# A decoder block with two-level expert routing: 160 tokens' experts gathered by row, sums over eight expert tiles, and the second norm moved into the operands

## The chip, the cores and the metric

The kernel runs on one core of a Trainium2 chip. The metric is the device time of one execution in microseconds (us); the median of the runs counts. TensorE (PE in the profile) multiplies matrices, VectorE (DVE), ScalarE (ACT) and GpSimd (POOL) work element by element, SyncE (SP) and POOL issue the transfers.

## The reference

There are 520 tokens (512 of a prompt and 8 samples) of width 2048, in fp32. A normalized input is projected, two kinds of windowed attention with gates follow, and the branches are joined and projected by `w_out`. The last part, which the change is about, is a layer of 16384 small experts, each one row of `u` and one row of `v`:

```
h = x + (sigmoid(ga) * ya + sigmoid(gb) * yb) @ w_out
hn = rmsnorm(h, norm2_w)
q = (hn @ wq).reshape(t, 8, 2, 64)            # 8 heads, two halves
s = einsum('thcd,cnd->thcn', q, subkeys)      # 128 scores for each half
half_s, half_i = top_k(s, 16)
best_s, best_c = top_k(all 256 sums of two halves, 16)
experts = i1 * 128 + i2;  gates = softmax(best_s)
act = gelu(einsum('cd,ced->ce', hn, u[experts]))
y = h + einsum('ce,ced->cd', gates * act, v[experts])
```

Each token thus uses 8 x 16 = 128 of the 16384 experts.

## The kernel before, in words

**Number format.** A weight tile of 128 x 2048 fp32 (1 MB) is fetched by SP into one of two raw buffers. In two halves of 1024 columns ACT rounds it to fp32r (`wh`, L297) and DVE subtracts to get the rest (`wl`, L299). Each product is three matmuls: wh with the rounded operand, wh with its rest, wl with the rounded operand. All matmuls of this kind have line L336. `plan` lists the weights in order, and `stream` starts the next tile's transfer and splitting one tile ahead.

**Stages.** By the trace's time: projections and attention until about 975 us; the branches until 1143; `wout` until 1389; the query products `wq` with the routing until 1826; the gates until 2179; the rest of the dense `u` tiles that are stored until 2286; then the experts until 3890. The last four hold the two ways in which expert products are made:

- *Dense*, for the first ND = 392 tokens. PE multiplies all 16384 rows: `u_tile` makes 128 experts x 392 tokens from 16 x 3 matmuls of 392 columns, a norm factor is multiplied in by DVE (L930), and ACT takes the gelu. The first 70 of the 128 tiles are computed while routing and gates run, and stored to DRAM (`act_d`); the rest are computed among the `v` products. The gates are spread out to a dense matrix by `build_g`: for every four tokens DVE compares indices with an iota (`eA`, `Bt`, L1097 and L1099), POOL and ACT multiply in the gate (`AA`), and PE makes the outer products (`gq`, L1080); it is stored as `g_d`. In the experts `c_tile` multiplies a tile by its gates (L1218) and splits it (`cb`, L1221). `v_group` sums GRP = 4 tiles in PSUM, for two chunks of 128 of the output's width at a time, and DVE adds the sum to `acc` (L1263).
- *Gathered*, for the last NS = 128 tokens. With one token on each partition, an indirect DMA of POOL fetches a row of `u` for each (128 x 2048, 1 MB, L1155); DVE multiplies it with the token and sums (`dot`, L1185). After 128 of these come 128 rows of `v`, which DVE adds with a weight (`add`, L1197). Three buffers take turns. At the end PE transposes the sums.

**Norm.** Before, HH and HL hold h times the norm's weight without the factor 1/rms. The factor `rstd` is made after the first query product and multiplied in where a product leaves PSUM.

**What sets the order.** Everything else is hung on PE's work: each matmul counts its columns, and each 16 x 260 columns is a *tick*. A tick advances one of up to three generators (top-16 searches, `build_g`, `gathered`); PACE = 3.1 is the ticks between two gathered rows. PE and SP run in the order of the code, in the experts POOL too; a scheduler places the instructions of the other engines. top-16 (`best_all`) runs token tile by token tile: the gathered tile of 128 first, then four of 98.

Of the kernel before, what the change touches and what calls it, by code (L numbers as in the profile page):

```python
# [49 lines left out]
KA = 12  # L50
NEXP = 128
NSPILL = 70
GRP = 4
TICK = 16
NACT = 3
COPY_EVERY = 9
# [3 lines left out]
NCB = 6  # L60
NGB = 3
PACE = 3.1
PRE = 2
LEAD = 3
# [27 lines left out]
def _layout(a):  # L92
# [12 lines left out]
    o["v"] = f["peer_v"][0].reshape(NEXP // GRP, GRP, P, 4, 2, 256).transpose(0, 3, 2, 4, 1, 5)  # L105
# [46 lines left out]
def _plan():  # L152
    p = [("win", 8 + i) for i in range(4)] + [("win", i) for i in range(8)]
    for j in range(NJ):
        for g in range(NG):
            p += [("win", b + g * 4 + j) for b in (12, 24, 36)]
    p += [("win", 48 + i) for i in range(32)]
    for c in range(0, KC, 2):
        p.append(("wba", c // 2))
        if c % 4 == 0:  # L160
            p.append(("wbb", c // 4))
    p += [("wout", i) for i in range(KC)] + [("wq", i) for i in range(PH)]
    p += [("uT", i) for i in range(NSPILL)]
    for g in range(NEXP // GRP):
        p += [("uT", i) for i in range(g * GRP + (g > 0), min(NEXP, g * GRP + GRP + 1)) if i >= NSPILL]
        p += [("v", (g, q)) for q in range(4)]
    return p


def _program(tc, I, O):  # L170
# [16 lines left out]
    onesR = cp.tile([P, P], F32R, name="onesR")  # L187
    V.tensor_copy(onesR, ones)
# [5 lines left out]
    eg = cp.tile([P, 2, P], F32, name="eg")  # L194
# [31 lines left out]
    act_d = dp.tile([NSPILL, P, ND], F32, name="act_d")  # L226
    g_d = dp.tile([NGC, P, NK, GC], F32, name="g_d")


    clock = {"n": 0}  # L230
    first, active, queue = deque(), deque(), deque()

    def soon(f, lag=1):
        first.append((clock["n"] + lag, f))

# [20 lines left out]
    def drain(all_=True):  # L256
        while first:
            first.popleft()[1]()
        while all_ and (active or queue):
            step()  # L260
# [161 lines left out]
    qk = sp = tab = sbias = qs = kn = vn = None  # L422
# [3 lines left out]
    def start_attention():  # L426
        nonlocal qk, sp, tab, sbias, qs, kn, vn
# [3 lines left out]
        sp = at.enter_context(tc.tile_pool(name="sp", bufs=1))  # L431
        tab = sp.tile([P, 512], F32, name="tab")
# [382 lines left out]
    oa = (lambda k: sl["OA"][:, k], lambda k: sl["OA"][:, 8 + k])  # L815
# [21 lines left out]
    for n in range(2):  # L837
        for c in range(KC):
# [35 lines left out]
    acc = slp.tile([P, KC, T], F32, name="acc", tag="S2")  # L874
    HHt = slp.tile([P, KC, ND], F32R, name="HH", tag="S3")
    HGt = slp.tile([P, KC, NS], F32R, name="HG", tag="S3g")
    ssq = bt.tile([P, T], F32, name="ssq")
    for c in range(KC):
        w = stream(("wout", c))
        if c < 4:  # L880
            S_.dma_start(acc[:, c * 4:c * 4 + 4, :], I["xT"][:, c * 4:c * 4 + 4, :])
        ps = psum_mm()
        dot3(ps, w, (mH, mL))
        V.tensor_tensor(v2(acc[:, c]), v2(acc[:, c]), ps[:, :, :TH], op=OP.add)
        w2 = cst[:, C_N2 + c:C_N2 + c + 1]
        A.activation(HHt[:, c], acc[:, c, :ND], AF.Copy, scale=w2)
        A.activation(HGt[:, c], acc[:, c, ND:], AF.Copy, scale=w2)
        if c == 0:
            A.activation(ssq, acc[:, c], AF.Square)
        else:  # L890
            s = tmp0()
            A.activation(s, acc[:, c], AF.Square)
# [4 lines left out]
    hg = (whole(HGt), whole(HLGt))  # L897
    for c in range(KC):
        w2 = cst[:, C_N2 + c:C_N2 + c + 1]
        V.scalar_tensor_tensor(HLt[:, c], acc[:, c, :ND], w2, HHt[:, c], op0=OP.mult, op1=OP.subtract)  # L900
        V.scalar_tensor_tensor(HLGt[:, c], acc[:, c, ND:], w2, HGt[:, c], op0=OP.mult, op1=OP.subtract)


    def q_product(h):
        w = stream(("wq", h))
        ps = psum_mm()
        terms([(ps[:, 0, :ND], 0, ND), (ps[:, 1, :NS], ND, T)],
              [pick(w, k * P) + tuple((d(k), g(k)) for d, g in zip(hw, hg)) for k in range(KC)])
# [29 lines left out]
    def spill_u():  # L938
        nonlocal nu
        act = u_tile(nu)  # L940
        G_.dma_start(act_d[nu], act)
# [7 lines left out]
    s1b = cp.tile([TT, 4096], F32, name="s1b", tag="S1b")  # L949
    hs = s1b[:, :HN].rearrange("p (t h c k) -> p t h c k", t=NTT, h=PH, c=2)  # L950
    hi = s1b[:, HN:2 * HN].bitcast(U32).rearrange("p (t h c k) -> p t h c k", t=NTT, h=PH, c=2)
    s1b0 = 2 * HN
    hf = s1b[:, s1b0:s1b0 + 256].rearrange("p (h c k) -> p h c k", h=PH, c=2)
    ab = s1b[:, s1b0 + 256:s1b0 + 512].bitcast(U32).rearrange("p (c x) -> p c x", c=2)
    abf = s1b[:, s1b0 + 768:s1b0 + 1024].rearrange("p (c x) -> p c x", c=2)
    pos_ = s1b[:, s1b0 + 512:s1b0 + 640]
    res = s1b[:, s1b0 + 1024:s1b0 + 1408].rearrange("p (c h k) -> p c h k", c=3, h=PH)
    qT = cp.tile([P, PH, T], F32, name="qT", tag="S1a")
# [11 lines left out]
    def halves_top(h):  # L970
        yield

        def score(t):
            t0, m = TILES[t]
            ps = sc_p.tile([P, 512], F32, name="sc")
            PE.matmul(ps[:m, :256], qT[:, h, t0:t0 + m], sk, start=True, stop=True)  # L976
# [16 lines left out]
    def best_all():  # L993
        s1a = cp.tile([TT, 4096], F32, name="s1a", tag="S1a")
# [16 lines left out]

        nxt = cand(0)
        yield
        yield
        for t in range(NTT):
            cur = nxt
            t0, m = TILES[t]
            for h in range(PH):
                top16(bs[:m, h], bc[:m, h * TOPK:(h + 1) * TOPK], cur[:, h], NC_)
                yield  # L1020
            if t + 1 < NTT:
# [34 lines left out]
            ps = sc_p.tile([P, 512], F32, name="sc")  # L1056
            for x in range(3):
                PE.transpose(ps[:, x * P:x * P + m], rows[:, x], ident[:m, :m])
            ts = slice(t0, t0 + m)
            V.tensor_copy(i1T[:, ts], ps[:, 0:m])  # L1060
            V.tensor_copy(i2T[:, ts], ps[:, P:P + m])
            A.activation(gH[:, ts], ps[:, 2 * P:2 * P + m], AF.Copy)
            V.tensor_tensor(gL[:, ts], ps[:, 2 * P:2 * P + m], gH[:, ts], op=OP.subtract)
            yield
        queue.append(build_g())


    def build_g():
# [257 lines left out]
```

## Time and profile before

| | |
|---|---|
| median of 3 runs | 3904.21 us (3903.19 to 3906.29) |
| profiled execution | 3891.22 us, its span 3889.5 us |
| PE busy | 3812.2 us (98%), 25080 matmuls |
| DVE, ACT, POOL busy | 2753.0 us (71%), 1436.4 us (37%), 930.5 us (24%) |
| TensorE's granted clock, mean | 0.993 of full speed |
| moved by DMA | 901.37 MB, mean 232 GB/s |

The profiled execution is 13.0 us below the median. The shares of busy time are means over stages that differ, so a stage's own window is to be read beside them. A busy PE is an engine with a matmul in flight. Durations of one instruction on DVE and POOL include the time in which it was held after its start.

### The profile page before, as it was taken

The numbers are of one execution on the slowest core, as the hardware profiler recorded it, in microseconds if no ns is written. First come the engines' busy times: TensorE is split into PE (matmuls) and PEld (weight loads), VectorE is DVE, ScalarE is ACT, GpSimd is POOL, SyncE is SP. The second block draws the span as 40 slices with busy tenths as digits, with TensorE's granted clock in tenths as the row PEclk, the third lists the DMA queues.
The fourth block names the chain that finished last, engine by engine and source line by source line (L and its number), as shares of the span: only waits on it lengthen the run. The fifth ranks groups of instructions, "written<-read, shape, count | busy, mean of one in ns | idle before, by whom it ended". The sixth has DMA issues, their size and how long they took to land.

```text
span 3889.5 us, 61269 instructions
## 1 busy us (share of the span) xinstructions
PE 3812.2 (98%) x25080; PEld 3779.9 (97%) x25080; DVE 2753.0 (71%) x3925; ACT 1436.4 (37%) x2032; POOL 930.5 (24%) x944
## 2 busy tenths in 40 slices
PE   8999999999999999989999999999999999999999
PEld 8999999999999999989999999999999999999999
DVE  5444333778654357898666579999988888888864
ACT  5655444222322322323777532222222323232232
POOL 2111111223210000133666322222222222222200
PEclk9999999999999999999999999999999999999999
DMA  4233334667656333545544579898888889888853
GB/s 164 103 113 137 141 133 183 222 242 260 228 202 236 141 132 116 191 162 197 199 187 184 201 297 336 319 332 318 333 329 330 318 329 337 331 312 304 331 209 131
DMA packets 140761, 901.37 MB, mean 232 GB/s; under 512 B 20096, under 2 KB 21088, under 8 KB 56512
## 3 DMA queue, kind: packets, MB, share of 16 engines
q1 hardware_dynamic: 59296, 489.74, 33.5%
q0 software_dynamic: 66064, 380.27, 26.4%
q10 hardware_dynamic: 15120, 27.43, 2.2%
q8 instruction: 198, 3.24, 0.3%
q14 instruction: 83, 0.68, 0.1%
HBM read 836.48 MB, written 150.95 MB: 254 GB/s over the span
## 4 chain that ended last, share of the span: by engine, by line
PE 84%; DVE 8%; issue 4%; DMA 2%; ACT 1%; POOL 0%; ACTq 0%; POOLq 0%; DVEq 0%
PE mm L336 71%; PE vv L336 8%; DVE wl L299 3%; PE gq L1080 2%; DVE gb L1185 1%; DMA k<-q_d 1%; PE sc L976 0%; ACT wh L297 0%; DMA wr<-in_win 0%; PE a L510 0%; DVE acc L1263 0%; PE a L517 0%; DVE s1b L1048 0%; PE a L523 0%; DVE c L1221 0%
## 5 line engine op out<-in xcount | busy, mean ns | idle before, releaser
L297 ACT ACTIVATE wh<-wr 128x1024 fp32r<-128x1024 f32 x744 | 787.4, 1059 | 1840.3 <-PE mm L336 1454.3
L299 DVE TENSOR_TENSOR wl<-wr,wh 128x1024 fp32r<-128x1024 f32 x744 | 948.3, 1279 | 335.8 <-ACT wh L297 334.0
L336 PE MATMUL mm<-HH,wl 128*128 128x392 f32 x2176 | 755.1, 347 | 15.3 <-DVE wl L299 15.3
L336 PE MATMUL mm<-HH,wh 128*128 128x392 f32 x2176 | 759.1, 349 | 2.1 <-ACT wh L297 1.2
L336 PE MATMUL mm<-HL,wh 128*128 128x392 f32 x2176 | 756.0, 347 | 0.0
L336 PE MATMUL mm<-c,wh 128*128 128x392 f32 x2316 | 608.5, 343 | 3.9 <-DVE c L1221 3.9
L336 PE MATMUL mm<-S,wh 128*128 128x260 f32 x3048 | 589.0, 285 | 8.2 <-ACT S L380 8.2
L336 PE MATMUL mm<-S,wl 128*128 128x260 f32 x2664 | 545.0, 286 | 5.3 <-DVE wl L299 5.3
L336 PEld LDWEIGHTS mm<-S,wh 128*128 128x128 f32 x3048 | 460.2, 190 | 10.4 <-ACT S L380 8.2
L336 PEld LDWEIGHTS mm<-c,wh 128*128 128x128 f32 x2316 | 426.1, 189 | 6.9 <-DVE c L1221 6.1
L336 PEld LDWEIGHTS mm<-HH,wl 128*128 128x128 f32 x2176 | 412.2, 189 | 19.3 <-DVE wl L299 18.6
L336 PEld LDWEIGHTS mm<-S,wl 128*128 128x128 f32 x2664 | 414.5, 190 | 8.8 <-DVE wl L299 5.7
L336 PEld LDWEIGHTS mm<-HH,wh 128*128 128x128 f32 x2176 | 411.5, 189 | 4.0 <-ACT wh L297 1.5
L336 PEld LDWEIGHTS mm<-HL,wh 128*128 128x128 f32 x2176 | 411.6, 189 | 0.9
L336 PE MATMUL mm<-c,wl 128*128 128x392 f32 x1158 | 396.0, 342 | 1.4 <-DVE wl L299 1.4
L336 PE MATMUL mm<-S1a,wh 128*128 128x260 f32 x1520 | 311.0, 286 | 4.2 <-DVE S1a L381 4.1
L336 PE MATMUL mm<-S1b,wh 128*128 128x260 f32 x1520 | 312.2, 287 | 2.1 <-DVE S1b L381 2.1
L336 PE MATMUL vv<-c,wh 128*128 128x392 f32 x1108 | 293.0, 344 | 8.7 <-DVE c L1221 5.5
L1197 DVE SCALAR_TENSOR_TENSOR hb<-gb,dots,hb 128x2048 f32<-128x2048 f32 x127 | 298.1, 2347 | 4.4 <-DMA gb<-in_vn,idx 4.3
L1185 DVE SCALAR_TENSOR_TENSOR gb<-gb,hb 128x2048 f32<-128x2048 f32 x128 | 292.6, 2286 | 3.1 <-DMA gb<-in_un,idx 3.1
L1155 POOL DMA_INDIRECT gb<-in_vn,idx x128 | 158.7, 1240 | 462.5 <-DVE hb L1197 397.3
L336 PEld LDWEIGHTS mm<-S1a,wh 128*128 128x128 f32 x1520 | 235.0, 189 | 6.2 <-DVE S1a L381 5.1
(317 smaller groups left out, 5584.8 us busy)
## 6 DMA issues: line engine op xcount, KB each, us to landing
wr<-in_uT SPq DMA_DIRECT2D x128, 1024.0 KB, 4.9
wr<-in_v SPq DMA_DIRECT2D x128, 1024.0 KB, 7.3
wr<-in_win SPq DMA_DIRECT2D x78, 1024.0 KB, 4.8
g_d<-stg POOLq DMA_DIRECT2D x14, 1792.0 KB, 6.9
ga<-g_d POOLq DMA_DIRECT2D x32, 784.0 KB, 10.8
wr<-in_wout SPq DMA_DIRECT2D x16, 1024.0 KB, 4.8
out_s<-in_c SPq DMA_DIRECT2D x16, 1020.0 KB, 7.3
act_d<-t POOLq DMA_DIRECT2D x70, 196.0 KB, 2.6
```

Of the source, the lines that this page charges most:

```text
L297: A.activation(h, r, AF.Copy)
L299: V.tensor_tensor(l, r, h, op=OP.subtract)
L336: PE.matmul(ps, u, y[lo >= ND][:, lo % ND:hi - lo + lo % ND] if isinstance(y, tuple) else y[:, lo:hi], start=(begin and i == 0 and a == 0) ...
L1080: PE.matmul(ps[:, t], Bt[:, t], AA[:, t, x], start=x == 0, stop=x == 1)
L1155: G_.indirect_dma_start(out=g, out_offset=None, in_=src, in_offset=bass.IndirectOffsetOnAxis(ap=idx[:, j:j + 1], axis=0))
L1185: V.scalar_tensor_tensor(g, g, 1.0, hn, op0=OP.mult, op1=OP.mult, accum_out=dots[:, j:j + 1])
L1197: V.scalar_tensor_tensor(sums, g, coef[:, j:j + 1], sums, op0=OP.mult, op1=OP.add)
```

## The change

Tokens: 360 go the dense way and 160 the gathered way. The 160 are two sets: 128 tokens with a row each on a partition as before, then 32 tokens that fill the 128 partitions four times over, a quarter of their 128 experts each, so that 32 rows of `u` and 32 of `v` do for them. Hence 160 + 160 rows are fetched in place of 128 + 128.

Order: routing takes the gathered tiles first, then three of 120 tokens. The rows begin when the first tile is routed, at a pace of their own for each stage (`PACES`), outside the three generators; POOL is in written order from there. The tokens' rows `hb` are made beforehand by transposes among the query products (`hn_rows`). For the rows in the stage routing, and for every second row in the stage experts, the product of `dot` is made by POOL, and ACT sums it; in the gates, and else, DVE does both as before.

Norm: `rms` comes ahead of the query products, and `rstd` is multiplied into HH and HL chunk by chunk. L930 and the factor in the queries are gone; the gelu reads PSUM, and ACT copies the queries. The first two query products run chunk by chunk side by side. `wout` is cut as 360 + 160 columns (before 260 + 260).

Sums: GRP is 8, so there are half as many adds to `acc`, of 128 x 720. Three of each eight tiles are computed among the `v` products and 80 are stored, where before the first 70 were. The buffers of `eA`, `Bt`, `AA` are three each. The transfers to `act_d` and `g_d` are issued three ticks after their data. What is left of the gathered work is done at once ahead of the last `v_group`.

The core of the diff:

```diff
-ND, NS = 392, 128
+ND, NS = 360, 160
+NA_, NB_, RB = 128, 32, 4
...
-TILES = [(ND, NS)] + [(i * (ND // 4), ND // 4) for i in range(4)]
-GC, NGC = 28, 14
...
-NSPILL = 70
-GRP = 4
+GRP = 8
+GL = 4
+INLINE = {g * GRP + i for g in range(NEXP // GRP) for i in (0, 3, 6)}
+SPILLED = [i for i in range(NEXP) if i not in INLINE]
+NSPILL = len(SPILLED)
...
-PACE = 3.1
-PRE = 2
-LEAD = 3
+PACES = {'routing': 4.0, 'gates': 3.5, 'u': 2.3, 'v': 2.9}
+LEAD = 2
+LAG = 2
...
+        while posts and posts[0][0] <= clock["n"]:
+            posts.popleft()[1]()
+        if pace and clock["n"] >= pace["due"]:
+            pace["due"] += next(pace["gen"], 1e9)
...
+    def cut2(ps):
+        return [(ps[:, 0, :ND], 0, ND), (ps[:, 1, :NS], ND, T)]
...
+        dot3(cut2(ps), w, (mH, mL))
+        s = tmp0() if c else ssq
+        for a, b, n in ((acc, 0, ND), (accg, 1, NS)):
+            V.tensor_tensor(a[:, c], a[:, c], ps[:, b, :n], op=OP.add)
+            A.activation(s[:, b * ND:b * ND + n], a[:, c], AF.Square)
...
+    psr = psum_mm()
+    rms(ssq, [psr[:, h, :TH] for h in range(2)])
+    rstd_ = rstd.rearrange("p h t -> p (h t)")
...
+        x = tmp1() if c % 2 else tmp0()
+        for a, lo, hi, h, l in ((acc, 0, ND, HHt, HLt), (accg, ND, T, HGt, HLGt)):
+            V.scalar_tensor_tensor(x[:, lo:hi], a[:, c], w2, rstd_[:, lo:hi], op0=OP.mult, op1=OP.mult)
+            A.activation(h[:, c], x[:, lo:hi], AF.Copy)
+            V.tensor_tensor(l[:, c], x[:, lo:hi], h[:, c], op=OP.subtract)
+    G_.dma_start(h_d, accg)
...
+    def q_products(hs):
+        ws = [stream(("wq", h)) for h in hs]
+        ps = [psum_mm() for _ in hs]
+        for k in range(KC):
+            for w, p in zip(ws, ps):
+                terms(cut2(p), [pick(w, k * P) + tuple((d(k), g(k)) for d, g in zip(hw, hg))], k == 0, k == KC - 1)
...
-        pre = tp.tile([P, ND], F32, name="t0", bufs=2)
-        V.tensor_tensor(pre, ps, rstd_[:, :ND], op=OP.mult)
         act = tp.tile([P, ND], F32, name="t1", bufs=2)
-        A.activation(act, pre, AF.Gelu)
+        A.activation(act, ps, AF.Gelu)
...
-        G_.dma_start(act_d[nu], act)
+        n, act = nu, u_tile(SPILLED[nu])
+        post(lambda: G_.dma_start(act_d[n], act))
...
+                cell["stage"] = "routing"
+                perm.enter_context(tc.manual_schedule(engines={mybir.EngineType.PE, mybir.EngineType.SP, mybir.EngineType.Pool}))
+                pace.update(gen=gathered(), due=clock["n"] + 2)
...
+    psq = q_products((0, 1))
...
+        homes = ((slp, "S3g"), (cp, "S0g"), (slp, "S2g"))
...
+                yield PACES[cell['stage'] if cell['stage'] in PACES else side]
+
+        for e, S, n, c0 in ((eg, P, NA_, NB_), (egb, P // RB, NB_, 0)):
...
+            def dot(j, g):
+                if cell["stage"] == "routing" or cell["stage"] == "experts" and j % 2:
+                    G_.tensor_tensor(g, g, hn, op=OP.mult)
+                    A.activation(g, g, AF.Copy, accum_out=dots[:, j:j + 1])
+                else:
+                    V.scalar_tensor_tensor(g, g, 1.0, hn, op0=OP.mult, op1=OP.mult, accum_out=dots[:, j:j + 1])
...
+            yield from rows("v", idx, S, add)
+            hx = buf()[:, :KC * n].rearrange("p (c t) -> p c t", c=KC)
+            G_.dma_start(hx, h_d[:, :, c0:c0 + n])
...
-        if i < NSPILL:
-            for k in range(len(acts), min(i + LEAD, NSPILL)):
-                acts.append(tp.tile([P, ND], F32, name=f"t{k % 2}", bufs=2))
-                G_.dma_start(acts[k], act_d[k])
-            act = acts[i]
-        else:
-            act = u_tile(i)
-        c_tile(i, act)
+        if i % GL == 0:
+            for x in (i // GL, i // GL + 1):
+                if x not in Gs:
+                    load_g(x)
+        if i in INLINE:
+            c_tile(i, u_tile(i))
+            return
+        n = SPILLED.index(i)
+        while len(acts) < LEAD:
+            load_act()
...
-        for dq in range(4):
-            w = stream(("v", (g, dq)))
-            for d2 in range(2):
-                dc = dq * 4 + d2 * 2
-                wh, wl = w[d2]
+        for dc in range(0, KC, 2):
+            w = stream(("v", (g, dc // 2)))
+            for _ in range(1):
...
+                    items = [pick(w, t * 256 + dl * P) + Cs[g * GRP + t] for t in range(GRP)]
...
-            cell["rush"] = True
-            drain()
+            for _ in pace["gen"]:
+                pass
```

What stands in the engines' queues before and after follows at three places. In the routing, POOL holds before the stores of the dense tiles (`act_d`) and the products of the index search (`s1a`):

```order
L941 DMA act_d<-t_17819 128x392
L1045 TENSOR_TENSOR s1a<-s1a,s1b 98x2048
L941 DMA act_d<-t_17893 128x392
L1045 TENSOR_TENSOR s1a<-s1a,s1b 98x2048
L941 DMA act_d<-t_17988 128x392
```

After, the gathered rows (`row...`, from `u`, here `in_un`) and their products with the token (`hb`) stand between them:

```order
L1235 DMA rowS0g<-in_un,idx 128x2048
L1254 TENSOR_TENSOR rowS2g<-rowS2g,hb 128x2048
L1089 TENSOR_TENSOR s1a<-s1a,s1y 120x2048
L969 DMA act_d<-t_19368 128x360
L1235 DMA rowS2g<-in_un,idx 128x2048
L1254 TENSOR_TENSOR rowS3g<-rowS3g,hb 128x2048
L1089 TENSOR_TENSOR s1a<-s1a,s1y 120x2048
```

A transfer and a product of 128 x 2048 have come in for each store. In the gates, DVE holds before the splitting (`wl`), the comparisons (`Bt`, `eA`) and the norm factor (`t`):

```order
L930 TENSOR_TENSOR t_20457<-mm,rstd 128x392
L299 TENSOR_TENSOR wl<-wr,wh 128x1024
L1099 TENSOR_TENSOR Bt<-cst,i2T 128x512
L1097 TENSOR_TENSOR eA<-cst,i1T 128x512
L1099 TENSOR_TENSOR Bt<-cst,i2T 128x512
L1097 TENSOR_TENSOR eA<-cst,i1T 128x512
L299 TENSOR_TENSOR wl<-wr,wh 128x1024
```

After, the norm factor is gone and a row's dot product stands among the comparisons:

```order
L315 TENSOR_TENSOR wl<-wr,wh 128x1024
L1157 TENSOR_TENSOR Bt<-cst,i2T 128x512
L1257 SCALAR_TENSOR_TENSOR rowS0g,dots<-rowS0g,hb 128x2048
L1155 TENSOR_TENSOR eA<-cst,i1T 128x512
L315 TENSOR_TENSOR wl<-wr,wh 128x1024
L1157 TENSOR_TENSOR Bt<-cst,i2T 128x512
L1155 TENSOR_TENSOR eA<-cst,i1T 128x512
```

One operation of 128 x 2048 has come in for about every second group of four tokens. In the experts, while rows of `u` are fetched, POOL holds before transfers alone (`t` from `act_d`, `ga` the gates, `gb` a row):

```order
L1232 DMA t_25330<-act_d 128x392
L1213 DMA ga<-g_d 128x14x112
L1232 DMA t_25336<-act_d 128x392
L1155 DMA gb_25356<-in_un,idx 128x2048
L1155 DMA gb_25397<-in_un,idx 128x2048
```

After, a product stands in front of every second row's transfer:

```order
L1235 DMA rowS3g<-in_un,idx 128x2048
L1254 TENSOR_TENSOR rowS0g<-rowS0g,hb 128x2048
L1235 DMA rowS0g<-in_un,idx 128x2048
L1235 DMA rowS2g<-in_un,idx 128x2048
L1254 TENSOR_TENSOR rowS3g<-rowS3g,hb 128x2048
L1235 DMA rowS3g<-in_un,idx 128x2048
```

The transfer into a buffer follows the product that reads the same buffer, so POOL's queue now holds work on the row beside the fetching of it.

## Rows read from the trace of the kernel before

**Rows 1.** The page: chain that ended last, by engine, and GB/s in 40 slices.

```profile
PE 84%; DVE 8%; issue 4%; DMA 2%; ACT 1%; POOL 0%; ACTq 0%; POOLq 0%; DVEq 0%
...
GB/s 164 103 113 137 141 133 183 222 242 260 228 202 236 141 132 116 191 162 197 199 187 184 201 297 336 319 332 318 333 329 330 318 329 337 331 312 304 331 209 131
```

**Rows 2.** Busy time in five stretches: us, then as the head says.

```profile
core 0: us, PE busy (x) PEld busy (x) DVE busy (x) ACT busy (x) POOL busy (x), PEclk, DMA share, GB/s
1387.00:1414.00 27.00, 20.35 (x124) 19.63 (x122) 16.39 (x36) 5.68 (x8) 0.00 (x0) 0.87 0.00 1
1640.00:1826.00 186.00, 170.15 (x901) 166.35 (x899) 185.21 (x414) 62.76 (x76) 69.02 (x36) 0.95 0.47 172
1826.00:2179.00 353.00, 352.30 (x2267) 352.26 (x2268) 233.53 (x292) 259.19 (x483) 229.66 (x239) 1.00 0.51 191
2286.00:2900.00 614.00, 591.37 (x3237) 583.41 (x3236) 557.26 (x593) 176.69 (x202) 164.99 (x176) 0.99 0.89 329
2900.00:3800.00 900.00, 900.00 (x5025) 899.20 (x5024) 761.34 (x651) 269.84 (x315) 196.87 (x163) 1.00 0.83 310
```

**Rows 3.** The chain, three runs of matmuls: start us, us, engine, group, count.

```profile
975.14 411.76 PE mm L336 x3432
...
1432.21 6.91 PE mm L336 x48
...
3339.98 42.94 PE mm L336 x240
```

**Rows 4.** Timeline around `rms`: start us, us, engine, line, operation, [idle before].

```profile
1413.16 0.84 ACT L366 ACTIVATE rstd<-mm,epst 128x260 f32<-128x260 f32 x2 [5.76 <-PE mm L364]
...
1415.31 0.64 ACT L367 ACTIVATE rstd<-rstd 128x520 f32<-128x520 f32 x1
```

**Rows 5.** Timeline of POOL and DVE at four places, columns as in rows 4.

```profile
786.91 6.25 POOL L732 TENSOR_TENSOR q<-q,k 128x512 f32<-128x512 f32 x5
...
787.06 7.18 DVE L299 TENSOR_TENSOR wl<-wr,wh 128x1024 fp32r<-128x1024 f32 x1
...
1690.90 4.61 POOL L1045 TENSOR_TENSOR s1a<-s1a,s1b 98x2048 f32<-98x2048 f32 x1 [2.42 <-DVE s1a L1043]
...
1691.16 4.50 DVE L1035 SCALAR_TENSOR_TENSOR s1b<-s1b 98x128 f32<-98x128 f32 x1
...
1900.57 1.04 POOL L1104 TENSOR_TENSOR AA<-eA,gL 128x512 fp32r<-128x512 bf16 x1
```

**Rows 6.** DVE, groups by shape, 1640 to 1826: busy us, mean ns, idle before.

```profile
L299 DVE TENSOR_TENSOR wl<-wr,wh 128x1024 fp32r<-128x1024 f32 x36 | 61.8, 1716 | 0.0
L1043 DVE TENSOR_TENSOR s1a<-s1b,cst 98x2048 f32<-98x2048 f32 x8 | 18.3, 2287 | 0.0
```

**Rows 7.** DVE and PE, groups by shape, whole span.

```profile
L1097 DVE TENSOR_TENSOR eA<-cst,i1T 128x512 bf16<-128x512 f32 x98 | 67.7, 691 | 89.8 <-POOL AA L1104 89.8
...
L1080 PE MATMUL gq<-AA,Bt 128*128 128x128 f32 x784 | 98.4, 268 | 0.0
```

**Rows 8.** DVE, POOL and ACT, groups by shape, 2300 to 2900.

```profile
L1185 DVE SCALAR_TENSOR_TENSOR gb<-gb,hb 128x2048 f32<-128x2048 f32 x97 | 221.7, 2286 | 0.0
L299 DVE TENSOR_TENSOR wl<-wr,wh 128x1024 fp32r<-128x1024 f32 x132 | 159.8, 1222 | 3.3 <-ACT wh L297 3.3
...
L1218 DVE TENSOR_TENSOR t<-t,ga 128x392 f32<-128x392 f32 x62 | 33.8, 562 | 1.5 <-DMA ga<-g_d 0.9 <-ACT t L932 0.6
...
L1155 POOL DMA_INDIRECT gb<-in_un,idx x97 | 110.1, 1135 | 259.8 <-DVE gb L1185 240.0 <-issue 12.4 <-DVE acc L1263 6.7
...
L297 ACT ACTIVATE wh<-wr 128x1024 fp32r<-128x1024 f32 x131 | 138.9, 1060 | 337.8 <-PE mm L336 218.3 <-PE vv L336 102.1 <-DMA wr<-in_v 7.8
```

**Rows 9.** DVE, groups by shape, 2900 to 3780.

```profile
L1197 DVE SCALAR_TENSOR_TENSOR hb<-gb,dots,hb 128x2048 f32<-128x2048 f32 x127 | 298.1, 2347 | 4.4 <-DMA gb<-in_vn,idx 4.3
```

**Rows 10.** DMA issues: operation, count, KB each, median us from issue to landing.

```profile
wr<-in_v SPq DMA_DIRECT2D x128, 1024.0 KB, 7.3
...
gb<-in_un,idx POOLq DMA_INDIRECT x128, 7.6
```

More of the change, by code (lines that the diff above doesn't have):

```diff
@@ L256, in drain @@
     def drain(all_=True):
[L257 to L260, printed above, removed]
+        while first or posts or all_ and (active or queue):
+            if first or posts:
+                (first or posts).popleft()[1]()
+            else:
+                step()
     copies = []
@@ L431, in start_attention @@
         sp = at.enter_context(tc.tile_pool(name="sp", bufs=1))
+        onesR = sp.tile([P, P], F32R, name="onesR")
+        V.tensor_copy(onesR, ones)
         tab = sp.tile([P, 512], F32, name="tab")
@@ L1010, in cand, with by_slot @@
             return c
+        def by_slot(t, rows):
+            t0, m = TILES[t]
+            ps = sc_p.tile([P, 512], F32, name="sc")
+            for x in range(3):
+                PE.transpose(ps[:, x * P:x * P + m], rows[:, x], ident[:m, :m])
+            ts = slice(t0, t0 + m)
+            V.tensor_copy(i1T[:, ts], ps[:, 0:m])
+            V.tensor_copy(i2T[:, ts], ps[:, P:P + m])
+            A.activation(gH[:, ts], ps[:, 2 * P:2 * P + m], AF.Copy)
+            V.tensor_tensor(gL[:, ts], ps[:, 2 * P:2 * P + m], gH[:, ts], op=OP.subtract)
         nxt = cand(0)
+        left = None
         yield
@@ L1020, in best_all @@
                 yield
+                if h == 4 and left:
+                    by_slot(*left)
+                    left = None
             if t + 1 < NTT:
@@ L1177, in gathered @@
-        for _ in range(4):
-            yield
-        hn = cpl.tile([P, D], F32, name="hb")
-        yield from turn(lambda c: hd[:, c],
-                        lambda q, ps: A.activation(hn[:, q * 1024:(q + 1) * 1024].rearrange("p (x n) -> p x n", x=2),
-                                                   ps, AF.Copy))
-        def dot(j, g):
-            V.scalar_tensor_tensor(g, g, 1.0, hn, op0=OP.mult, op1=OP.mult, accum_out=dots[:, j:j + 1])
-        yield from rows(I["un"], dot)
-        coef = dots
@@ L1207, in gathered @@
-        yield from turn(lambda c: sums[:, c * P:(c + 1) * P], put)
+                    k = q * 8 + c
+                    PE.transpose(ps[:, c // 4, (c % 4) * P:(c % 4) * P + P], sums[:, k * P:(k + 1) * P], ident)
+                dst = hx[:, q * 8:q * 8 + 8]
+                part = ps.rearrange("p x (c n) -> p (x c) n", c=4)
+                for r in range(P // n):
+                    V.tensor_tensor(dst, dst, part[:, :, r * n:(r + 1) * n], op=OP.add)
+                yield 1
+            G_.dma_start(O["y"][:, :, ND + c0:ND + c0 + n].rearrange("c p t -> p c t"), hx)
@@ L1283, in _program @@
         start_experts()
-    perm.enter_context(tc.manual_schedule(engines={mybir.EngineType.PE, mybir.EngineType.SP, mybir.EngineType.Pool}))
-    queue.append(gathered())
+        load_g(0)
+        load_g(1)
+        cell["stage"] = "experts"
+    while nu < NSPILL:
+        spill_u()
+        if cell.get("stage") != "experts" and not active and not queue:
+            begin()
+    if cell.get("stage") != "experts":
+        drain()
+        begin()
+    drain(False)
     c_of(0)
```

297 lines of the change are left out of this document (150 added, 147 removed).

## The prediction, made before the result was known

> **What bounds the kernel now.** I read the chain of waits first, then the busy time by stretches, then DVE's and POOL's groups and timelines in the stretches that the change touches. PE makes 84% of the chain [rows 1], so PE's work counts one for one wherever PE is never kept waiting. The stretches show where that holds [rows 2]: from 2900 to 3800 PE is busy without a gap, in the gates (1826 to 2179) for 352.30 of 353 us. It does not hold in three places. At the step from `wout` to the query products 124 matmuls fill some 18 of 27 us: 9 lost. In the routing (1640 to 1826) 901 matmuls at 0.179 us (below) fill 161 of 186: 24 lost. While rows of `u` are gathered (2286 to 2900), 3237 matmuls fill 579 of 614: 35 lost. There DVE is the busiest, 185 of 186 and 557 of 614 us.
>
> Why DVE: it and POOL do not work side by side on what lies in SBUF. A split of DVE that takes 1.22 us elsewhere [rows 8] took 7.18 beside POOL products in a row, and ended 1.08 us after the last of them; a small DVE operation started 0.26 us after a POOL product of 4.61 us, took 4.50 and ended 0.15 us after it [rows 5]. So I count what each operation needs of this shared path ("the port"): its record less 0.14 us. That is 1.08 for a split, 2.15 for a row's dot product on DVE [rows 8] or an index product [rows 6], 4.47 for a product of POOL and 0.90 for `AA` [rows 5], 0.55 for `eA` [rows 7] and as much for `Bt`, which is alike.
> The Trainium skill (SBUF — State Buffer, section "SBUF: two separate sides") calls this an exclusive lock held for the whole instruction, whose loser fully blocks. The trace agrees on the block, but not on one instruction's length: the split of 7.18 us stood behind five products. By the page alone each waiter would lose one instruction at most, and the result would lie nearer the first rival's time.
>
> **The change part by part**, against the profiled execution of 3891.2 us.
>
> *PE's own work.* A matmul of 392 columns follows the last after 42.94 / 240 = 0.1789 us, one of 260 after 411.76 / 3432 = 0.1200, so 0.446 ns a column, and 360 columns take 0.1646 [rows 3]. The experts have 256 x 48 = 12288 of these: 12288 x 14.3 ns = −176. `wout` has 768 pairs of 260 + 260 (0.240), now 360 + 160. No row has 160 columns: the slope gives 75 ns, 260 columns bound it at 120. A pair of 392 + 128 took 6.91 / 48 x 2 = 0.288 us, so 109 ns for its short part, and I take 110 as the nearest: 768 x 0.0346 = +27 (0 to +34). The query products have 384 pairs: −5. `gq` takes (352.3 − 1483 x 0.1789) / 784 = 0.111 us [rows 2, 7]; 64 fewer are −7. More transposes: +3. Together −158.
>
> *`wout` to the queries.* The norm comes ahead now: a last add, square and sum, two matmuls with ones, then ACT's two logarithms, table load and exponential, 2.8 us [rows 4], with handovers some 7.5. Then DVE feeds the first two products chunk by chunk, about 30 us for PE's 26.4, and the clock, 0.87 over this stretch before [rows 2], costs 0.13 x 20 us of matmuls less what stands idle anyway, some 2. 7.5 + 3.7 + 2 = 13 against 9: +4 (0 to +15).
>
> *Routing.* The first tile is alone, about 5 lost. Then 20 `u` tiles (158 us of PE) cover 18 POOL products (80), 8 index products on each engine (17 and 36), 40 splits (43) and 10 of small things: 186 on the port, +28. If POOL's 116 stand in line with all of DVE's work, it is 226: before, DVE was busy 185, of which its 36 splits waited 18 [rows 6] and its operations beside ten products of POOL some 30 [rows 5], so 137 for five tiles, 110 for four. That is +68. I take +45, midway: DVE was busy throughout here while the port needed only some 112 (36 x 1.08 + 10 x 2.15 + 10 x 4.47 + 7), which speaks against the port alone. So 50 lost in place of 24: +26.
>
> *Gates.* 32 `u` tiles and 720 `gq` take PE 253 + 80 = 333. Port, for each four tokens `eA`, `Bt`, `AA` and a quarter of `AA`: 90 x (0.55 + 0.55 + 0.90 + 0.24) = 202, 64 splits = 69, 38 dot products = 82, together 352: +19. With whole records of both engines in line, 90 x (0.69 + 0.69 + 1.04 + 0.26) + 64 x 1.22 + 38 x 2.29 = 406: +73. Before, the same sum (98 of the first, and 32 norm factors at 0.55 for the dots) was 358 in 353 and nothing was lost, so I stay by the port: +22 (0 to +60). The norm factor that goes (L930) reads PSUM, and its 0.55 us a tile free DVE and not the port; I cost that at nothing.
>
> *Rows of `v`, and the old place of the dots.* The 35 lost before from 2286 to 2900 go with that stretch: −35; what takes its place is counted next. 160 rows of `v` at 2.9 ticks (4160 columns, 11.56 matmuls, 1.90 us) take 904 us with the ends. For each, DVE has an add of 2.35 [rows 9], 1.40 splits and 1.0 of other things: 5.05 in 5.52 us, 91.5%; by the same terms 90% before, where nothing was lost. +7 (0 to +40). Half as many adds to `acc` are within that.
>
> *Rows of `u` in the experts.* For 59 rows at 2.3 ticks PE has 258 us. Port: 65 splits = 70, 48 gate products and rests at 0.39 = 19 (0.56 less 0.14, for 360 columns [rows 8]), 28 dot products = 60, 31 POOL products = 139: 288, +30. POOL itself needs, for two rows, two issues of 1.135 [rows 8], a product of 4.61, then ACT's sum before the buffer is fetched into again (2.1 from twice the ACT copy of 1024 columns [rows 8]), a handover of 0.6 and 0.8 for the lock: 10.4, or 5.2 a row, 307: +49. Behind the product wait the next row's fetch and the stored tiles' loads (`t`) in the same queue, and for those PE. I take +48. The second set's 32 rows: PE 140, port 154, POOL 166: +24. Bounds for both, by the port and by all records in line: +44 to +84.
>
> *End.* The last sums' 16 transposes stand just ahead of the last 384 matmuls, and wait for the last add and each other: +6 (2 to 12).
>
> Sum: −158 + 4 + 26 + 22 − 35 + 7 + 72 + 6 = −56: 3835 for a profiled execution. The median lies 13.0 above the profiled one before, so 3848.
>
> **The rivals.**
> *Only the port counts.* Everything that the port doesn't need runs beside it, and POOL's cycle overlaps: routing 28, gates 19, `u` rows 30 + 14, `v` rows 0. That is 55 less: 3793. For it: nothing was lost in the gates with both engines' records filling the time. Against: from 2286 to 2900 the port had room and 35 were lost.
>
> *Transfers.* With 1 MB every 5.52 us for a row (190 GB/s), 11 MB of weights every 87 us (132) and 2.4 MB of stored tiles and gates (28), the `v` rows ask for 350 GB/s, for `u` rows 400. The highest slice is 337 and the long stretches have 310 to 329 [rows 1, 2]. If 329 to 336 is a ceiling, the 904 us grow by 38 to 58, and the gain goes down to about 8: 3896, no change. For it: the slices look level at 330. Against: rows landed after 7.6 us and weights after 7.3, with three and two buffers [rows 10], and PE set the pace there.
> The Trainium skill (DMA: Bandwidth & Descriptors, section "Specifications") gives about 358 GB/s between HBM and one core. By it 350 fits, so the `v` rows would stretch by nothing and the sum stays; no run here has shown more than the slice of 337.
>
> *POOL's products stand in line with all of DVE's SBUF work* (slower). Then routing loses 68 beside tile 0, the gates 60 and the `u` rows 84: 212 in place of the 139 above, 3921. It decides once these stretches lose over some 195 together, since all else gives −158 + 4 + 5 − 24 − 35 + 7 + 6 = −195. For it: the 7.18 us split, behind five products. Against: the gates before.
>
> That narrower matmuls don't take less time is held off by rows 3 and gets 1%, within the slower case.
>
> **How the numbers follow.** Forecast 3848: 0.42; the port alone, 3793: 0.26; transfers, 3896: 0.12; in line, 3921: 0.20. This kernel's measurement can tell about 0.2%, 7.8 us. Faster by more: 0.39 + 0.26 + 0.04 + 0.02 = 0.71; within: 0.02 + 0.04 + 0.02 = 0.08; slower: 0.01 + 0.04 + 0.16 = 0.21. The range goes from under the first rival, where a 160-column matmul of 75 ns would take off another 40 (3753), to above the last: 3760 to 3950. The forecast's own range is 3815 to 3885.
>
> **What would show it.** Matmuls of 360 columns in undisturbed stretches 0.165 us apart; pairs in `wout` at 0.27 to 0.28. PE's idle time in routing some 50 us, in the gates some 20, in the `u` rows of the experts 70, under 10 in the `v` rows; there DVE's splits of 2 to 6 us beside POOL products, and POOL idle before a fetch for ACT's sum. Wrong would be: level GB/s at 330 with PE waiting for splits that wait for their transfer (the transfers), or wide PE gaps in the gates (all in line).

## The result, and the profile after

The changed kernel takes 4045.64 us (median of 4; 4042.32 to 4051.28) against 3903.97: ratio 1.0363, 95% interval 1.0345 to 1.0381. It is slower by 3.6%; the forecast was 3848. The profiled execution has a span of 4045.9 us. The page after, its busy times, granted clock and transfers:

```profile
PE 3736.8 (92%) x25045; PEld 3674.6 (91%) x25045; DVE 2862.2 (71%) x3651; ACT 1578.0 (39%) x2176; POOL 1505.6 (37%) x1103
...
PEclk9999999999999999998899998889999999999899
...
GB/s 160 123 140 148 148 150 182 260 281 232 241 230 208 137 120 105 147 174 201 181 269 287 286 327 271 289 284 289 352 312 321 346 354 332 330 278 288 306 347 153
```

PE is busy 75 us less than before, and the span is 156 longer. With each matmul at the usual time for its width, PE's work went from 3741.0 to 3591.8 us, 149 less; what is lost beside it went from 135 to 441. So PE's work did shrink, and much more came in as standing still and as slow matmuls. Narrow matmuls are as forecast: the chain after has 240 of 360 columns in 39.62 us, 0.165 each (before, 392 columns [rows 3]):

```profile
3854.69 39.62 PE mm L352 x240
```

Where it stands, by stretches (columns as in [rows 2]: us, busy of PE, PEld, DVE, ACT, POOL, clock, DMA share, GB/s): the step from `wout`, the routing with rows, the gates, the first set's rows of `u` in the experts, its rows of `v`, the second set's rows of `u`.

```profile
1433.00:1470.00 37.00, 26.43 (x162) 24.79 (x161) 30.09 (x72) 19.43 (x42) 0.54 (x1) 0.82 0.44 164
...
1750.00:1990.00 240.00, 178.82 (x999) 173.83 (x999) 209.39 (x310) 94.34 (x116) 163.25 (x77) 0.87 0.52 190
1990.00:2368.00 378.00, 352.14 (x2286) 345.26 (x2285) 373.37 (x319) 277.15 (x453) 322.73 (x270) 0.97 0.75 275
...
2434.00:2817.00 383.00, 301.12 (x1648) 290.59 (x1648) 306.71 (x212) 149.06 (x173) 247.21 (x119) 0.89 0.75 279
2817.00:3561.00 744.00, 715.60 (x4272) 710.41 (x4271) 614.53 (x509) 229.60 (x271) 263.98 (x187) 0.99 0.88 335
3576.00:3797.00 221.00, 182.71 (x1018) 175.59 (x1018) 176.31 (x121) 84.95 (x97) 135.82 (x68) 0.92 0.77 284
```

Rows of `u` now leave PE without work for a fifth of their stretch, at a clock of 0.89 and 0.92. Before, it was busy 591 of 614 us there [rows 2]. "Lost" below is, summed over the matmuls of a stretch, the time to the next one beyond the usual time for its width (0.165 us for 360 columns, 0.179 for 392); for the first set's rows of `u` that is 383 − 1648 x 0.165 = 111.

| stretch (before; after) | lost before | lost after | forecast after |
|---|---|---|---|
| step to the queries (1387 to 1414; 1433 to 1470) | 10 | 15 | 13 |
| routing, first tile's search included (1640 to 1826; 1700 to 1990) | 27 | 78 | 50 |
| gates (1826 to 2179; 1990 to 2368) | 0 | 40 | 22 |
| rows of `u` in the experts (2286 to 2900; 2434 to 2817 and 3576 to 3797) | 35 | 165 | 72 |
| rows of `v` (2900 to 3800; 2817 to 3561 and 3797 to 3968) | 1 | 48 | 7 |
| last sums (from 3800; from 3968) | 1 | 8 | 7 |

How one loss comes about, in the first set's rows of `u` (start us, us, engine, line, operation, [idle before]):

```profile
2531.92 4.60 POOL L1254 TENSOR_TENSOR rowS3g<-rowS3g,hb 128x2048 f32<-128x2048 f32 x1
...
2532.19 5.42 DVE L315 TENSOR_TENSOR wl<-wr,wh 128x1024 fp32r<-128x1024 f32 x1 [1.10 <-ACT wh L313]
...
2535.03 0.49 PE L352 MATMUL mm<-c8S1x,wh 128*128 128x360 f32 x2
...
2537.66 0.43 PE L352 MATMUL mm<-c8S1x,wl 128*128 128x360 f32 x1 [2.15 <-DVE wl L315]
...
2539.14 0.80 PE L352 MATMUL mm<-cb,wh 128*128 128x360 f32 x2
...
2542.45 0.49 PE L352 MATMUL mm<-c8S1b,wh 128*128 128x360 f32 x2
```

A split of 1.22 us stands behind POOL's product and ends 1.1 us after it; PE waits 2.15 us for it. Then, from 2538.4 to 2541.8, two matmuls take 0.80 where they took 0.49 before and after: 1.2 GHz for 2.4; the granted clock from 2538.6 to 2542.0 is 0.51. The gap is paid a second time. From the first gate product to the first add of `v`, 87 of 115 us are in gaps over 1 us, and some 19 of the other 27 are such slow matmuls.

At a group's start the same comes in a row, since up to five stored tiles are multiplied and split there:

```profile
2579.53 5.20 DVE L1298 TENSOR_TENSOR c8S1b<-t,c8S1b 128x360 fp32r<-128x360 f32 x1
2579.83 4.51 POOL L1254 TENSOR_TENSOR rowS2g<-rowS2g,hb 128x2048 f32<-128x2048 f32 x1
...
2585.56 1.14 POOL L1320 DMA_DIRECT2D t<-act_d  x2
...
2589.32 4.52 POOL L1254 TENSOR_TENSOR rowS0g<-rowS0g,hb 128x2048 f32<-128x2048 f32 x1
2590.46 4.67 DVE L1295 TENSOR_TENSOR t<-t,ga 128x360 f32<-128x360 f32 x3 [3.52 <-DMA ga<-g_d]
...
2595.28 1.45 PE L352 MATMUL vv<-c8S1y,wh 128*128 128x360 f32 x2 [8.62 <-ACT c8S1y L1297]
```

The loads `t` stand behind the product in POOL's queue, the gate product behind the next one at the port, and PE waits 8.62 us.

### The profile page after: what moved, and what is told of

Same layout as the page of the kernel before. It is cut to its first block, busy times and chain, and to the rows that moved or that the text cites. A ratio compares the mean times of both kernels' runs of the same rounds, so it can differ in the third digit from the quotient of the medians.

```text
span 4045.9 us, 61363 instructions
## 1 busy us (share of the span) xinstructions
PE 3736.8 (92%) x25045; PEld 3674.6 (91%) x25045; DVE 2862.2 (71%) x3651; ACT 1578.0 (39%) x2176; POOL 1505.6 (37%) x1103
## 5 line engine op out<-in xcount | busy, mean ns | idle before, releaser
L352 PE MATMUL mm<-HH,wl 128*128 128x360 f32 x2176 | 734.6, 338 | 57.4 <-DVE wl L315 57.2
L352 PE MATMUL mm<-HH,wh 128*128 128x360 f32 x2176 | 731.5, 336 | 10.0 <-ACT t L960 5.3
L352 PE MATMUL mm<-HL,wh 128*128 128x360 f32 x2176 | 729.7, 335 | 1.8 <-DVE HL L928 1.8
L352 PE MATMUL mm<-S,wh 128*128 128x260 f32 (+2 forms) x2698 | 540.0, 288 | 7.9 <-ACT S L396 7.9
L352 PE MATMUL mm<-S,wl 128*128 128x260 f32 (+2 forms) x2474 | 513.2, 289 | 7.1 <-DVE wl L315 6.8
L352 PE MATMUL mm<-c8S1b,wh 128*128 128x360 f32 x1120 | 284.9, 335 | 28.8 <-ACT c8S1b L1297 27.9
L352 PE MATMUL mm<-cb,wh 128*128 128x360 f32 x1072 | 273.2, 337 | 7.3 <-ACT cb L1297 7.2
L352 PE MATMUL mm<-S1b,wh 128*128 128x260 f32 (+1 forms) x1140 | 238.7, 291 | 1.8 <-DVE S1b L397 1.8
L352 PE MATMUL mm<-S1a,wh 128*128 128x260 f32 (+1 forms) x1140 | 238.6, 291 | 1.5 <-DVE S1a L397 1.4
L352 PEld LDWEIGHTS mm<-c8S1b,wh 128*128 128x128 f32 x1120 | 203.9, 193 | 31.8 <-ACT c8S1b L1297 29.5
```

The source lines that it names most:

```text
L352: PE.matmul(ps, u, y[lo >= ND][:, lo % ND:hi - lo + lo % ND] if isinstance(y, tuple) else y[:, lo:hi], start=(begin and i == 0 and a == 0) ...
```

## The experiments

The kernel before was measured again beside each group of these runs, at medians of 3895 to 3897 us; ratios are against that. Differences to the changed kernel's 4045.6, whose own run had 3904 beside it, hold to some 8 us.

**POOL's products in the experts.** Label e1_dve.

```
-                if cell["stage"] == "routing" or cell["stage"] == "experts" and j % 2:
+                if cell["stage"] == "routing":
```

> The changed kernel, but in the experts every row's dot product is made by DVE alone (POOL makes its products in the routing only). Theory P (POOL's products of 4.6 us are what holds DVE's splits and gate products back in the rows of u in the experts): PE's loss there, 113 + 54 us in the changed kernel, falls to some 40 + 15, time about 3935 us. Rival D (the rows come too densely, whoever multiplies; DVE would then be full): the loss stays over 130, time 4010 to 4060.

Measured 3918.78 us, ratio 1.0044 (1.0027 to 1.0061): 127 us less than the changed kernel. From the first gate product to the first add, and between the two sets' adds (a little more than the table's stretches), 31 and 23 us are lost in place of 115 and 59. Theory P holds, and D falls as the main cause. The edit takes ACT's sums of these rows away with POOL's products, so this run doesn't say what the sums alone cost. DVE's splits in 2434 to 2810 after, and in 2417 to 2735 of this run (busy us, mean ns):

```profile
L315 DVE TENSOR_TENSOR wl<-wr,wh 128x1024 fp32r<-128x1024 f32 x66 | 152.1, 2313 | 47.7 <-ACT wh L313 46.9 <-issue 0.8
```

```profile
L315 DVE TENSOR_TENSOR wl<-wr,wh 128x1024 fp32r<-128x1024 f32 x72 | 87.1, 1222 | 26.5 <-ACT wh L313 26.2
```

And that stretch of this run, as in the table of stretches:

```profile
2417.00:2735.00 318.00, 295.28 (x1732) 291.10 (x1731) 270.90 (x287) 96.48 (x120) 114.03 (x89) 0.97 0.91 349
```

Every split is back at 1.222 us [rows 8], and about as many rows (60 dot products for 61) come through in 318 us for 383, at 349 GB/s.

**Cache copies.** Label e2_copy9: `COPY_EVERY = 9` in place of 7.

> The changed kernel with the cache copies issued every 9 ticks as before (7 in the changed kernel). In the changed kernel the first dense u tile is split 16 us later than the same work's terms give, and those 16 us are lost in projections and attention, where no code but the copies' rate was meant to change. Theory C (denser copies delay the attention's transfers): the 16 us come back, 4030 us. Rival S (the scheduler's new order of DVE, ACT and POOL there): no change, 4046 us within 5.

4050.43 us, ratio 1.0394 (1.0376 to 1.0412): no gain, so theory C falls. Rival S falls too: the first branch weight is split at 1053 to 1073 us in the fourteen profiled executions of this case, in which this part's work is the same (1056.7 in before, 1072.9 after, 1058.6 here). The 16 us belonged to that execution.

**No rows.** Label e5_norows: the generator of rows is empty.

```
-                pace.update(gen=gathered(), due=clock["n"] + 2)
+                pace.update(gen=iter(()), due=clock["n"] + 2)
```

> The changed kernel without any gathered row: no fetch, no dot product, no add, no end of it (the 160 tokens' expert part is left out). All else stays. It prices the rows as a whole. Theory P and rival D both say that nearly all of the new loss is the rows': routing loses 25 in place of 60, gates 8 in place of 46, experts under 20 in place of 230, time about 3770 us. Rival B (sums over eight tiles: five stored tiles in a burst at each group's start, with two load buffers, lose time without the rows too): over 100 us lost in the experts, time 3850 or more.

3701.65 us, ratio 0.9503 (0.9487 to 0.9518). Without rows the experts lose 3 us in all: rival B falls, sums over eight tiles cost nothing by themselves. The rows cost 344 us.

**No rows, before.** Label b0_norows: `queue.append(gathered())` left out of the kernel before.

> The kernel before without any gathered row (no fetch, dot product, add or transposes of them; the 128 tokens' expert part is left out). It prices the rows of before, as the run without rows priced those of the changed kernel (344 us for 320 rows). By the stretches of before its rows cost some 38 us in rows of u, nothing in rows of v, and 5 to 8 for transposes: 3850 us. Then the dense part alone became some 150 us shorter by the change, as the forecast had it, and only the rows are to blame. Rival: the dense part gained less, and this time is 3800 or under.

3855.68 us, ratio 0.9897 (0.988 to 0.9913). Rows cost 40 us before. The dense part became 3855.7 − 3701.7 = 154 us shorter; the whole loss, 344 − 40 = 304, lies in the rows.

**Loads past POOL.** Label e4_loads:

```
-        G_.dma_start(acts[-1], act_d[len(acts) - 1])
+        A.dma_start(acts[-1], act_d[len(acts) - 1])
...
-        G_.dma_start(gm, g_d[:, :, g * GL:(g + 1) * GL, :].rearrange("c p i t -> p c (i t)"))
+        A.dma_start(gm, g_d[:, :, g * GL:(g + 1) * GL, :].rearrange("c p i t -> p c (i t)"))
```

> The changed kernel with the loads of the stored tiles and of the gates (t, ga) issued by ACT's queue in place of POOL's; POOL's products stay. Rival Q (the 7 to 10 us gaps at the groups' starts are loads that stand behind POOL's products and fetches in POOL's queue): these gaps go, 60 to 75 us less, about 3975 us. Theory P (the gaps are DVE's gate products held by POOL's products): 4046 us within 20.

4021.13 us, ratio 1.031 (1.0286 to 1.0333): 25 less. The gaps of 7 to 10 us in the experts become 4 to 5, but more of them. In the rows of `u` (first gate product to first add, and between the adds) 89 and 45 us are lost in place of 115 and 59, so there the queue is near a quarter, and the rest stays with POOL's products still in. But in the rows of `v` 96 are lost in place of 44, which hides most of that gain in the time; why was not looked into.

**The cut of `wout`.** Label e6_wout, on top of e1_dve:

```
-        dot3(cut2(ps), w, (mH, mL))
+        dot3(ps, w, (mH, mL))
...
+                V.tensor_tensor(a[:, c, :TH], a[:, c, :TH], ps[:, 0, :TH], op=OP.add)
+                V.tensor_tensor(a[:, c, TH:], a[:, c, TH:], ps[:, 1, :ND - TH], op=OP.add)
```

> The kernel with all of the experts' dot products on DVE (3919 us), and besides with wout cut as 260 + 260 columns as before (the adds to acc and accg are cut at 260 and 360). The term of the cut was +27 us, and the trace after shows 210.7 against 184.2 us for wout: 3892 us. Rival: three adds for a chunk in place of two delay the buffers of PSUM and take some of it back: 3900 to 3910.

3878.50 us, ratio 0.9954 (0.9938 to 0.9970). `wout`, from its first split to that of the queries, goes from 210.7 to 184.7 us: −26. The median went down 40; the other 14 are within what executions of these kernels differ by (3871 to 3887 here).

**No POOL product at all.** Label e7_alldve, on top of e1_dve: the routing's condition is `False`.

> The kernel with all of the experts' dot products on DVE (3919 us), and the routing's too: POOL makes no product of a row at all. Theory P (a product of POOL costs the port 4.47, one of DVE 2.15, wherever it stands): the routing loses 50 in place of 68, 3900 us. Rival F (in the routing DVE is full with the search, busy 209 of 240 us, so its 18 dot products of 2.3 us come on top): 3930 to 3955 us.

3874.79 us, ratio 0.9951 (0.9935 to 0.9968), 44 less. Theory P again; F falls though DVE is as busy (208.8 of the routing's 221 us, 210.6 of 243 in e1_dve). Routing and gates lose 20 and 13 us less.

**A slower pace.** Label e8_slow, on top of e1_dve: one set only, `'u': 3.1, 'v': 4.0`.

> The kernel with all of the experts' dot products on DVE, without the second set of rows (the 32 tokens' expert part is left out), and with the first set's rows slower in the experts: one in 3.1 ticks for u (2.3) and in 4.0 for v (2.9). Theory D (what is left of the rows' price in the experts, 34 + 48 us for the first set, comes from their density): under 15 us lost in the experts, and with the second set's 24 + 13 + 5 and its fetches gone about 3800 us. Rival G (each row has its price, some 0.4 to 0.6 us, at any pace): 70 to 80 lost, 3860 to 3875 us.

3836.39 us, ratio 0.9844 (0.9828 to 0.9861). The experts lose 11 in rows of `u` and 14 in rows of `v`, 30 in all; at the denser pace the first set alone had lost 31 and 45. That is nearer D than G; the time lies between the two, as routing and gates kept their price and the forecast of 3800 had left out part of it.

**Both edits.** Label e9_both: e6 and e7 together.

> Both edits that helped together: no product of a row on POOL anywhere (3875 us), and wout cut as 260 + 260 columns (27 us less in the trace, 40 in the medians). If they are independent, 3875 - 27 to 40 = 3835 to 3848 us, faster than the kernel before (3896) by 1.2 to 1.6%. Rival: with the wout term gone the rest meets a tighter place and less comes through: 3855 or more.

3870.84 us (3862.37 to 3880.81), ratio 0.9940 (0.9926 to 0.9954): the rival. `wout` kept its 26 us, but in the profiled executions what follows it took 22 more than in e7. I can't say why; these kernels differ by 10 to 20 us between executions.

**Products in pieces.** Label e10_pieces:

```
-                    G_.tensor_tensor(g, g, hn, op=OP.mult)
+                    for x in range(0, D, 512):
+                        G_.tensor_tensor(g[:, x:x + 512], g[:, x:x + 512], hn[:, x:x + 512], op=OP.mult)
```

> The changed kernel with each of POOL's products of a row cut into four instructions of 512 columns, with the same work in all. Theory P1 (a waiting DVE operation gets the port when the POOL instruction that holds it ends): waits of a split beside a product fall from up to 4.6 to some 1.2 us, the 7 to 10 us gaps shrink, about 3980 us. Theory P2 (the waiting one stays behind through POOL instructions in a row, as the split of 7.18 us did before): no gain, 4046 us or some more for the starts of the instructions, and splits of 5 us remain.

4071.99 us, ratio 1.0455 (1.0440 to 1.0470): P2 by the time. POOL's four pieces and the split that started beside them:

```profile
2514.36 4.98 POOL L1255 TENSOR_TENSOR rowS0g<-rowS0g,hb 128x512 f32<-128x512 f32 x4
...
2514.27 6.16 DVE L315 TENSOR_TENSOR wl<-wr,wh 128x1024 fp32r<-128x1024 f32 x1 [0.74 <-ACT wh L313]
```

The split ends at 2520.43, 1.09 us after the last of four pieces (2519.34). Three ends of POOL instructions let nothing of it through. So it went in 39 of the 51 products of the experts: a DVE operation that had come before the third piece's end was let in only at the end of the fourth. In 11 others the two took turns, as P1 has it, and the four pieces took 5.6 to 9.5 us:

```profile
2540.21 3.45 DVE L315 TENSOR_TENSOR wl<-wr,wh 128x1024 fp32r<-128x1024 f32 x2
...
2540.89 9.46 POOL L1255 TENSOR_TENSOR rowS2g<-rowS2g,hb 128x512 f32<-128x512 f32 x4
...
2544.26 1.65 DVE L315 TENSOR_TENSOR wl<-wr,wh 128x1024 fp32r<-128x1024 f32 x1 [0.59 <-ACT wh L313]
2545.83 3.38 DVE L1258 SCALAR_TENSOR_TENSOR rowS3g<-rowS3g,hb 128x2048 f32<-128x2048 f32 x1
```

In all 11 a split or dot product of DVE had begun 0.5 to 1.2 us before the first piece, but so it had, up to 0.6 us before, in some of the 39. What decides between the two is not shown.

**Rows later.** Label e11_late, on top of e9_both: `PACES = {'routing': 78.0, 'gates': 3.5, 'u': 2.2, 'v': 2.65}`.

> The kernel with both edits, but the rows pause in the routing (a first row, then none for 78 ticks) and come more densely in the experts (u every 2.2 ticks for 2.3, v 2.65 for 2.9). In the routing the 20 rows cost 33 us, 1.6 each. Theory D (what a row costs rises with density: in the experts 0.3 at 2.9 ticks, 0.6 at 2.3): 20 rows more there cost 35 to 50, so within 15 us of the kernel with both edits. Rival H (a row in the routing is dear for the search beside it, and the experts have room): 20 to 30 us faster.

3889.76 us, ratio 0.9984 (0.9973 to 0.9995), 19 slower than e9_both. Routing and gates lose 33 and not 89, the first set's rows of `u` 70 and not 35, and 14 rows are left over: a gap of 52.7 us ahead of the last group. The test is not clean, so it was tried again with less left over.

**Rows later, all done in time.** Label e12_pace: `'routing': 60.0` and `'v': 2.5`.

> As the run with the pause in the routing, with a shorter pause (60 ticks) and v rows every 2.5 ticks, so that about 14 more rows are done before the end. In that run 14 rows were left over and were done in one gap of 52.7 us ahead of the last v group, while routing and gates lost 55 us less than in the kernel with both edits. Theory H2 (the pause is a gain, and the gap hid it): the gap falls under 10 us, a few us are lost again in gates and experts, 3845 to 3858 us. Theory D (density eats it): 3865 to 3885 us.

3872.04 us, ratio 0.9939 (0.9927 to 0.9952). The gap is gone. Routing and gates lose 53, the first set's rows of `u` 66 and of `v` 50 (89, 35 and 42 in e9_both): what is saved early is paid later. D.

## Why the prediction was wrong

**What held.** PE's own work and the step to the queries were −158 + 4 = −154; the two kernels without rows differ by −154. That it fits to the us is luck in part: PE's own work alone changed by −149 and the step by +5. `wout` was +27 and measures 210.7 against 184.2 in the trace, 26.5; its 768 pairs take 0.274 us each, as forecast. Neither the transfers' rate nor sums over eight tiles are to blame: e1_dve moved 349 GB/s over 318 us, above the slice of 337 on which the transfer rival stood. The page of that run:

```profile
GB/s 165 111 135 155 150 154 195 237 271 281 217 226 235 146 144 80 139 172 185 187 232 275 281 284 371 349 364 350 338 316 312 345 341 352 312 283 363 341 328 167
```

The Trainium skill's 358 (DMA: Bandwidth & Descriptors, section "Specifications") was passed by it a little, with slices of 371, 364 and 363; so that figure was no ceiling here either.

**Where the forecast was short.** A profiled execution was to be 56 us shorter and was 156 longer, 212 off. Of these some 93 are in the rows of `u` in the experts, 40 in the rows of `v`, 26 in the routing, 18 in the gates, 9 in PE's own work, 16 in projections and attention (that execution, e2_copy9), and 10 in stretches between.

**What failed: the term of the rows of `u` in the experts**, "I take 48" and +24, 72 together, 165 measured. POOL's cycle was the right mechanism, at 5.2 us a row; 61 rows took 376 us, 6.2 each. POOL's groups in 2434 to 2810 after show what was left out:

```profile
L1254 POOL TENSOR_TENSOR rowS0g<-rowS0g,hb 128x2048 f32<-128x2048 f32 x11 | 50.5, 4590 | 4.0 <-DMA rowS0g<-in_un,idx 3.8
...
L1235 POOL DMA_INDIRECT rowS2g<-in_un,idx x20 | 29.8, 1489 | 48.6 <-ACT rowS2g L1255 34.7 <-DVE rowS2g L1257 11.8 <-issue 1.2
L1235 POOL DMA_INDIRECT rowS3g<-in_un,idx x20 | 28.8, 1439 | 36.8 <-ACT rowS3g L1255 32.1 <-issue 1.8 <-DVE rowS3g L1257 1.6
L1235 POOL DMA_INDIRECT rowS0g<-in_un,idx x20 | 27.8, 1388 | 26.4 <-ACT rowS0g L1255 18.5 <-DVE rowS0g L1257 4.9 <-issue 2.1
L1320 POOL DMA_DIRECT2D t<-act_d x17 | 9.9, 585 | 20.2 <-DVE c8S1b L1298 13.6 <-DVE cb L1298 3.6 <-DVE c8S1y L1298 2.5
```

An issue takes 1.39 to 1.49 for 1.135 [rows 8]; POOL waited 85 us for ACT's sums, 2.75 for each of 31 products where I had 2.1; it also waits for the DVE dot products of the other rows and, before loads, 20 us for DVE's splits. The loads and their waits were named as what queues behind and not put into the cycle. Some of those waits are on DVE, which waits for POOL at the port, so the two slow each other, and I had taken the longest of PE, port and POOL as a stretch's time. That they lengthen each other is how I read these rows; no run took the one wait away without the other. Adding them up would not have been enough: my bound for all records in line was 84 for both sets. And I had no term for the clock after each gap in this stretch (some 19 of 115 us).

**Rows of `v`**: +7, measured 48. Busy DVE of 91.5% against 90% was read as room. Of the 14 gaps of PE over 1 us after the first add, 3 (of 2.15 to 4.01 us) follow a row that landed late; this is the longest:

```profile
2998.82 2.35 DVE L1268 SCALAR_TENSOR_TENSOR hb<-rowS0g,dots,hb 128x2048 f32<-128x2048 f32 x1 [4.95 <-DMA rowS0g<-in_vn,idx]
3001.09 2.35 DVE L315 TENSOR_TENSOR wl<-wr,wh 128x1024 fp32r<-128x1024 f32 x2
3002.36 0.43 PE L352 MATMUL mm<-HH,wl 128*128 128x360 f32 x1 [4.01 <-DVE wl L315]
```

DVE stands 4.95 us for a row that has not landed, two splits are behind the add, and PE waits. The other 11, of 1.8 us, have another order of DVE's before them: the add of PE's sums to `acc`, and behind it two splits, for the first of which PE waits:

```profile
2940.29 0.90 DVE L1342 TENSOR_TENSOR acc<-acc,mm 128x720 f32<-128x720 f32 x1 [2.35 <-PE mm L352]
2941.12 2.35 DVE L315 TENSOR_TENSOR wl<-wr,wh 128x1024 fp32r<-128x1024 f32 x2
2942.39 0.43 PE L352 MATMUL vv<-c8S1b,wl 128*128 128x360 f32 x1 [1.80 <-DVE wl L315]
```

In 7 of the 11 two adds of rows had just kept DVE busy, in 4 it stood waiting for PE. At one row in 4.0 ticks (e8_slow) 14 are lost in all, against 45 for the same set at 2.9 (e1_dve).

**Gates**, +22: 40 lost, all of it the rows' (none without them); within the range given for it. **Routing**, 50: 78 lost. Of its two bounds, "in line" (5 + 68 = 73) was the nearer, and even that was passed; POOL's products were part of it, as 20 us came back in e7_alldve. **The end**, +6, was 7.

**The rivals.** The slower one had the right sign with 3921 and is 125 short; its 212 was the sum of bounds that I took to be upper ones, with 7 for the rows of `v`. The first rival's rule of one instruction of waiting, which the Trainium skill's section "SBUF: two separate sides" (SBUF — State Buffer) would give, is contradicted by e10_pieces in most of its products: a waiter stood behind four instructions, 6.16 us for a split of 1.22. In 11 of 51 it did wait for one piece at a time.

**What is open.** Of the 344 us that rows cost, POOL's products account for 127 (e1_dve) and 44 (e7_alldve), so 171. About 173 stay in e7_alldve (3874.8 − 3701.7), for 320 rows on DVE. Against e5_norows that kernel loses 33 us more in the routing, 30 in the gates, and in the experts 48 in the rows of `u` and 45 in the rows of `v`, where e5_norows loses 3 in all. Pace moves it (e8_slow, e12_pace), but how much is DVE's time, the order of its queue or late landings was not separated.

## What to carry to other kernels

Price work moved to an engine that shares a path with the loaded one by what the other's instructions then wait, and put into its cycle every instruction of its queue, loads and their waits included. Where two engines wait for each other, the larger of their times is a lower bound; here even the sum of all their records fell short (84 us lost for 165). Side work that nearly hides in one arrangement (40 us for 256 rows) can cost many times that in a denser one (344 for 320, about half of it POOL's products), so measure the main work once without the side work and once with it.

## What was not expected of the hardware

Cutting a POOL product of 2048 columns into four mostly did not let DVE in between them (6.16 us for a split of 1.22, e10_pieces; so in 39 of 51 products, while in 11 they took turns). And a PE gap of 2.15 us, after matmuls without a pause, was followed by 3.4 us of matmuls at 1.2 GHz (0.30 us apart for 0.165), while another of 2.15, at 3097 us in the rows of `v`, was followed by none. Of the gaps of 1.8 us there, those at 3020 and 3399 were followed by 3.4 us at 1.2 GHz, and those at 2940, 3131 and 3220 by none. So the length of the gap alone does not tell it.
